# Weight operands of the up projection's first two output tiles formed during the input projection and kept in memory; the sample's residual loaded behind a group of shares

## The chip, the cores and the metric

The kernel runs on one core of a Trainium2 chip. Its engines work side by side: TensorE (PE, with its weight loads as PEld), VectorE (DVE), ScalarE (ACT), GpSimd (POOL) and SyncE (SP, which mostly issues transfers). Each has a queue of its own that it works through in order. The metric is the device time of one launch in microseconds.

## The reference

One layer of a decoder trunk, for a prompt of 1024 tokens and a sample group of 8 sequences with 8 tokens each, 1088 columns in all, in float32. The model width is 1024.

```python
h = rms_norm(x, norm1) * (1 + scale1) + shift1
z = h @ w_in              # q, kc, vc, ks, vs, kw, vw, gates, conv inputs, pooling input
...                       # compressed, selected and window attention; short convolution; pooling
x = x + gate1 * (concat([o_attn, y_conv, y_pool]) @ w_out)
h = rms_norm(x, norm2) * (1 + scale2) + shift2
a, b = split(h @ w_up, 2)                    # w_up: 1024 x 5632
x = x + gate2 * ((silu(a) * b) @ w_down)     # w_down: 2816 x 1024
```

The compressed attention needs the past keys and values, read from a paged cache: blocks of 32 positions go through `silu(flat @ w1) @ w2`.

## The kernel before

Channels lie on the partitions, columns on the free axis. A float32 product is made as three TensorE products of rounded parts: each operand is split into `hi` (a ScalarE copy, line 165) and `lo = operand - hi` (a VectorE subtraction, line 161), and hi x hi, lo x hi and hi x lo are summed in one bank (line 136).

The two big stages of the feed-forward part and the output projection use a scheme with seven products for eight blocks (`PRODUCTS`, `DOWN_PRODUCTS`). For the up projection one output tile j has a weight block of two 512 KB halves `w_raw` (from `in_wup`). From its four quarters seven weight operands are made: two are quarters as they stand, five are sums or differences of two (`w_s`, on GpSimd or VectorE), and each of the seven is split into `w_hi` and `w_lo` (`unit_weights`, seven pieces of 128x512, nine buffers). The columns go in two halves p0 and p1, each with its own operands `b_hi` and `b_lo`, again partly from sums `b_t` (on GpSimd): 7 operands for each of 4 channel groups, 28 per half. A pass (j, p) is 7 products x 4 channel groups x 3 = 84 matmuls of 128x272.

`ffn` makes the passes in the order (0,p0), (1,p0), (2,p0), (2,p1), (1,p1), (0,p1), then (3,p0), (3,p1), (4,p0) and so on. Passes in a row with the same j form a run and share weights, so the first runs are: run 0 = j 0 at p0, run 1 = j 1 at p0, run 2 = j 2 at p0 and p1, run 3 = j 1 at p1, run 4 = j 0 at p1. Tiles 0 and 1 are thus loaded and formed twice. The pieces of run n + 1 are formed during run n. p0's columns are ready first; p1's norm (`n_ss` on line 161, `n_rs` on 1472, `x1b` on 1478 to 1485) and operands come while p0's passes run. The combination of the products is `f_m`, `f_v`, `f_g` (lines 1557 to 1587).

The input projection goes tile by tile, in the order kc, vc, cg0, ch0, bg0, cg1, ch1, bg1, p0, ks, kw, p1, q0 to q3 (here p0 and p1 are two tiles of pooling input, not the halves of the columns). A tile is 24 matmuls for each of three column ranges. Between them a planner written in the kernel weaves in other work: `compress_more` (the compression: SP and GpSimd gather cache pages into `stream`, sixteen `stream` matmuls per step, then `vt`, a silu on ScalarE, and `vt,c_w`) and `late_ada` (`wada` loads and matmuls). The planner keeps an estimated time per engine and emits the step that it thinks ready first; `hold` lets a tile loop wait in the planner while other steps are emitted, and `spawn` starts such a step with a lead. The emitted order is the order of each engine's queue. Behind a pooling tile come running sums on VectorE (`pe_s`, `pe_x`, lines 837 to 857), the product `pe_x,pw` on TensorE, and `py` on ScalarE (line 866), stored to `mix_d`.

In the down projection each product ends in a share: ScalarE writes `d_m` (`down_share`, line 1768) and GpSimd adds it to `x`, or VectorE adds it directly (`down_gate`, line 1758). `down_run` loads the residual of the prompt in four pieces `x2[c]` on SP (line 1821) and that of the sample, `x2s`, on ScalarE's queue:

```python
if e == 1 and h == p == 0:
    nc.scalar.dma_start(xs, self.x1_d[:, :, SEQ:])     # line 1843
```

`issue_after` binds an instruction to stand behind another one in the emitted order.

## Time and profile before

| | before |
|---|---|
| median of 3 runs | 1695.42 us (1692.73 to 1697.64) |
| profiled execution | 1697.3 us |
| its span in the trace | 1695.7 us |
| granted TensorE clock, mean | 0.982 of full speed |
| busy: TensorE / VectorE / ScalarE / GpSimd | 1605.4 / 1122.6 / 819.0 / 680.1 us |

The span runs from the first to the last recorded instruction; 1.6 us of the execution's time lie outside it. The stages stand at these places of the span: input projection about 83 to 366 us, attention to 822, output projection to about 945, up projection to 1446, down projection to the end. The granted clock is the part of full speed that TensorE was given; its two levels are 1.2 and 2.4 GHz, and a stretch at 0.77 is a mix of them.

### The profile page before, as it was taken

What the parts mean: (1) busy time and instruction counts of PE and PEld (TensorE: products, weight loads), DVE (VectorE), ACT (ScalarE), POOL (GpSimd) and SP (SyncE); (2) the same over time, 40 slices, a digit from 0 to 9 for tenths busy, and PEclk for the clock granted to TensorE, in tenths of its full rate; (3) what the DMA queues carried; (4) which work ended last, traced back from release to release, by engine and by line L of the source; (5) the groups of instructions that cost most, each with busy time, mean ns of one, the idle gap of its engine ahead of it and who ended that gap; (6) DMA issues with size and microseconds to landing.
All of it is one profiled execution on the core that took longest, in us unless ns stands there. A gap on an engine that the chain in (4) does not pass through costs nothing.

```text
span 1695.7 us, 34350 instructions
## 1 busy us (share of the span) xinstructions
PE 1605.4 (95%) x11961; PEld 1409.9 (83%) x11961; DVE 1122.6 (66%) x2852; ACT 819.0 (48%) x1884; POOL 680.1 (40%) x797
## 2 busy tenths in 40 slices
PE   6999999998998999999899879999999999899988
PEld 2999997887766566666599769999999999899988
DVE  4603326685664866767689987776777776477695
ACT  3512225245766767666675644433333333344462
POOL 3101110022332322232216486544555554688695
PEclk9999999998999999999999989999999999999999
DMA  9555565216654644432673224436444445967553
GB/s 339 175 190 178 154 207 156 70 63 196 191 168 135 199 130 143 140 111 84 205 247 113 70 70 142 162 132 218 144 142 144 144 144 198 357 256 260 191 170 120
DMA packets 177327, 282.11 MB, mean 166 GB/s; under 512 B 25297, under 2 KB 113938, under 8 KB 176834
## 3 DMA queue, kind: packets, MB, share of 16 engines
q1 hardware_dynamic: 157282, 252.28, 45.5%
q0 software_dynamic: 5856, 16.24, 3.0%
q10 hardware_dynamic: 14016, 11.41, 2.2%
q8 instruction: 95, 1.56, 0.4%
q14 instruction: 78, 0.64, 0.1%
HBM read 220.85 MB, written 63.19 MB: 168 GB/s over the span
## 4 chain that ended last, share of the span: by engine, by line
PE 70%; DVE 12%; DMA 6%; ACT 4%; issue 3%; POOL 2%; SPq 1%; ACTq 0%; POOLq 0%; DVEq 0%
PE bank L136 65%; PE bank L140 5%; DVE w_lo L161 3%; DVE b_lo L161 1%; DMA wada<-in_wada 1%; DMA stream<-in_cacheA 1%; SPq L518 1%; DVE x L1758 1%; DMA w_raw<-in_wup 1%; POOL w_s L161 1%; DVE n_ss L161 1%; ACT w_hi L165 1%; DMA stream<-in_wtok 1%; DMA w_raw<-in_wout 1%; ACT stream L151 1%
## 5 line engine op out<-in xcount | busy, mean ns | idle before, releaser
L136 PE MATMUL bank<-b_hi,w_hi 128*128 128x272 f32 x1232 | 354.5, 293 | 12.9 <-DVE f_v L1557 4.6
L136 PE MATMUL bank<-b_lo,w_hi 128*128 128x272 f32 x1232 | 355.7, 290 | 3.2 <-DVE b_lo L161 3.2
L136 PE MATMUL bank<-b_hi,w_lo 128*128 128x272 f32 x1232 | 351.0, 290 | 1.3 <-DVE w_lo L161 1.3
L136 PEld LDWEIGHTS bank<-b_hi,w_hi 128*128 128x128 f32 x1232 | 232.5, 190 | 18.7 <-ACT b_hi L165 5.1
L136 PEld LDWEIGHTS bank<-b_lo,w_hi 128*128 128x128 f32 x1232 | 234.3, 190 | 4.8 <-DVE b_lo L161 4.6
L136 PEld LDWEIGHTS bank<-b_hi,w_lo 128*128 128x128 f32 x1232 | 232.3, 190 | 2.5 <-DVE w_lo L161 2.3
L1051 POOL TENSOR_SCALAR P<-P,st 128x128 f32<-128x128 f32 (+12 forms) x192 | 112.1, 593 | 262.3 <-DVE st L1049 87.3
L161 DVE TENSOR_TENSOR w_lo<-w_raw,w_hi 128x512 fp32r<-128x512 f32 (+2 forms) x129 | 125.2, 978 | 94.7 <-ACT w_hi L165 94.1
L161 POOL TENSOR_TENSOR w_s<-w_raw 128x512 f32<-128x512 f32 (+1 forms) x106 | 149.6, 1412 | 71.2 <-DVE w_lo L161 53.5
L165 ACT ACTIVATE w_hi<-w_raw 128x512 fp32r<-128x512 f32 (+2 forms) x130 | 86.4, 674 | 138.3 <-PE bank L136 88.5
L161 DVE TENSOR_TENSOR w_lo<-w_s,w_hi 128x512 fp32r<-128x512 f32 (+1 forms) x144 | 134.7, 940 | 19.5 <-ACT w_hi L165 15.1
L136 PE MATMUL bank<-stream 128*128 128x128 f32 x1056 | 133.5, 284 | 7.0 <-DMA stream<-in_cacheA 6.7
L136 PEld LDWEIGHTS bank<-stream 128*128 128x128 f32 x1056 | 128.1, 198 | 14.2 <-issue 9.7
L161 POOL TENSOR_TENSOR x<-x,d_m 128x272 f32<-128x272 f32 x144 | 125.6, 894 | 35.7 <-DVE x L1758 22.9
L136 PE MATMUL bank<-h_hi,w_hi 128*128 128x384 f32 (+1 forms) x384 | 130.8, 341 | 2.4 <-ACT py L866 2.3
L136 PE MATMUL bank<-g,w_hi 128*128 128x272 f32 x616 | 122.3, 294 | 8.4 <-ACT d_m L1768 6.7
L1043 ACT ACTIVATE P<-P,st 128x128 f32<-128x128 f32 (+12 forms) x192 | 113.2, 591 | 30.3 <-DVE st L1034 15.6
L136 PE MATMUL bank<-h_hi,w_lo 128*128 128x384 f32 (+1 forms) x384 | 127.2, 331 | 0.0
L136 PE MATMUL bank<-h_lo,w_hi 128*128 128x384 f32 (+1 forms) x384 | 126.7, 330 | 0.0
L136 PE MATMUL bank<-g,d_hi 128*128 128x272 f32 x616 | 118.7, 290 | 3.7 <-DVE x L1758 3.1
L165 ACT ACTIVATE w_hi<-w_s 128x512 fp32r<-128x512 f32 (+1 forms) x144 | 88.5, 620 | 66.6 <-PE bank L136 36.0
L1758 DVE SCALAR_TENSOR_TENSOR x<-bank,mod,x 128x272 f32<-128x272 f32 (+1 forms) x192 | 87.2, 476 | 42.2 <-PE bank L136 34.5
(369 smaller groups left out, 3855.0 us busy)
## 6 DMA issues: line engine op xcount, KB each, us to landing
g_d<-f_s SPq DMA_DIRECT2D x57, 544.0 KB, 3.4
g<-g_d SPq DMA_DIRECT2D x56, 544.0 KB, 7.9
wada<-in_wada SPq DMA_DIRECT2D x96, 256.0 KB, 5.5
stream<-in_cacheA SPq DMA_DIRECT2D x192, 128.0 KB, 3.4
w_raw<-in_wup SPq DMA_DIRECT2D x48, 512.0 KB, 4.3
unit<-in_cacheB SPq DMA_DIRECT2D x152, 128.0 KB, 2.4
stream<-in_cacheB SPq DMA_DIRECT2D x104, 128.0 KB, 2.3
w_raw<-in_wout SPq DMA_DIRECT2D x24, 512.0 KB, 4.9
```

The source lines that it names most:

```text
L136: return self.nc.tensor.matmul(out, lhsT, rhs, start=start, stop=stop, skip_group_check=chain)
L140: self.nc.tensor.transpose(out, in_, self.ident)
L151: self.nc.scalar.activation(out, in_, AF.Copy)
L161: (self.nc.vector if eng == "dve" else self.nc.gpsimd).tensor_tensor(out, a, b, op=op)
L165: self.nc.scalar.activation(hi, src, AF.Copy)
L518: eng.dma_start(dst[:, a + j, :], self.i[name][bass.ds(regs[j], 1)].rearrange("n p f -> (n p) f"))
L1043: nc.scalar.activation(Ps, Ps, AF.Exp, scale=-1.0, bias=sy[:, 0:1], accum_out=sy[:, 1:2])
L1051: nc.gpsimd.tensor_scalar(Ps, Ps, sy[:, 3:4], 0.0, op0=OP.mult, op1=OP.add)
L1758: nc.vector.scalar_tensor_tensor(out[:, :n], acc[:, :n], self.mod[:, 5, m, 0:1], out[:, :n], op0=OP.mult, op1=OP.add)
```

## The change

- `up_weights_ahead` loads the weight block of tile j, forms its seven pieces and stores them to a tile `w_d` in device memory: seven stores of 512 KB. Tile 0 is formed beside kc and vc, tile 1 beside q0 to q3. A hold behind each (`formed`) keeps the next tiles back until its steps have been emitted.
- `unit_weights` loads `w_hi` and `w_lo` of tiles 0 and 1 from `w_d`, 256 KB each, in place of loading and forming them: runs 0, 1, 3 and 4, 56 loads.
- kw comes behind p1, and the pooling of p1 has to be done before q0.
- The load of `x2s` is bound behind the last share that was emitted before it. On ScalarE it then stands behind the 24 shares of the first group of the down projection, where it stood behind two.

```diff
+AHEAD_W = 2
...
-        order = ["kc", "vc", "cg0", "ch0", "bg0", "cg1", "ch1", "bg1", "p0", "ks", "kw", "p1", "q0", "q1", "q2", "q3"]
+        order = ["kc", "vc", "cg0", "ch0", "bg0", "cg1", "ch1", "bg1", "p0", "ks", "p1", "kw", "q0", "q1", "q2", "q3"]
...
-            yield from tiles(["kc", "vc"], kcv)
+            with self.pool("pre") as pp:
+                self.spawn(0.6, self.up_weights_ahead(pp, 0))
+                yield from tiles(["kc", "vc"], kcv)
+                yield from self.hold(lambda: self.formed == 1)
             nc.gpsimd.dma_start(self.o["kcvcT"], self.kcv)
...
             with self.pool("pooling") as pl:
                 self.pooled = 0
-                for j, names in ((0, ["ks", "kw"]), (1, ["q0", "q1", "q2", "q3"])):
+                for j, names in ((0, ["ks"]), (1, ["kw"])):
                     step = self.pooling_steps(pl, j)
                     yield from tiles(["p" + str(j)], lambda nm, ch, acc, c0, n: step(ch, acc))
                     yield from tiles(names, qk)
                     yield from self.hold(lambda: self.pooled > j)
-                yield from self.hold(lambda: self.prompt_at and self.pooled == 2 and self.heads == 18 and 5 in self.ada_at)
+            with self.pool("pre") as pp:
+                self.spawn(0.6, self.up_weights_ahead(pp, 1))
+                yield from tiles(["q0", "q1", "q2", "q3"], qk)
+                yield from self.hold(lambda: self.formed == 2)
+            yield from self.hold(lambda: self.prompt_at and self.heads == 18 and 5 in self.ada_at)
...
+    def up_weights_ahead(self, pool, j):
+
+        nc = self.nc
+        raw = pool.tile([P, 2, D], F32, name="p_raw")
+        for x in range(2):
+            nc.sync.dma_start(raw[:, x], self.i["wup"][j, x])
+        at = self.use("dma", 2.9, self.t["pe"]) + 2.0
+        src = self.up_operands(raw[:, 0], raw[:, 1])
+        last = None
+        for y, x in enumerate(PRODUCTS):
+            yield at
+            t = pool.tile([P, 2, 512], F32R, name="p_hl", bufs=2)
+            v = src[x][0]
+            if len(src[x]) == 3:
+                v = t[:, 1].bitcast(F32)
+                at = self.combine(v, *src[x], 512, at, "pool")
+            at = self.split(t[:, 0], t[:, 1], v, 512, at)
+            if last:
+                nc.sync.dma_start(*last)
+            last = (self.w_d[j, :, y], t.bitcast(F32))
+        yield at
+        nc.sync.dma_start(*last)
+        self.formed += 1
...
-    def unit_weights(self, wp, j, raw, out):
+    def up_operands(self, ra, rb):
...
+    def unit_weights(self, wp, n, raw, out):
...
+        if isinstance(raw[n], int):
+            for y in range(7):
+                parts = [wp.tile([P, 512], F32R, name=nm, bufs=9) for nm in ("w_hi", "w_lo")]
+                for x in range(2):
+                    nc.sync.dma_start(parts[x].bitcast(F32), self.w_d[raw[n], :, y, x])
+                out.append((*parts, self.use("dma", 1.45, self.t["pe"]) + 2.0))
+                yield
+            return
...
-                raw[n] = tuple(self.weight_load(wp, self.i["wup"][runs[n][0], x]) for x in range(2))
+                j = runs[n][0]
+                raw[n] = j if j < AHEAD_W else tuple(self.weight_load(wp, self.i["wup"][j, x]) for x in range(2))
...
                     if e == 1 and h == p == 0:
-                        nc.scalar.dma_start(xs, self.x1_d[:, :, SEQ:])
+                        with self.tc.issue_after(self.last_share.ins):
+                            nc.scalar.dma_start(xs, self.x1_d[:, :, SEQ:])
...
+        self.w_d = self.dram.tile([AHEAD_W, P, 7, 2, 512], F32, name="w_d")
+        self.formed = 0
```

`up_operands` holds the table of sums and differences that `unit_weights` had.

How the change moves instructions is shown at three places, before and after. The names in brackets are the engines and transfer queues that an instruction waits for. The first place is TensorE behind the tile vc. Before: a step of the compression, `wada`, then the tile cg0 (`h_hi`, `h_lo`).

```order
L136 MATMUL bank<-stream 128x128 [waits DMAHW1_49,DMAHW2_49,DMAHW0_49,DMAHW7_49,DMASW7_49,DMASW0_49]
L136 MATMUL bank<-stream 128x128 x15
L136 MATMUL bank<-wada,sc 32x256 [waits DMAHW6_49]
L136 MATMUL bank<-wada,sc 32x256 [waits DMAHW7_49]
L136 MATMUL bank<-wada,sc 32x256 [waits DMAHW0_49]
L136 MATMUL bank<-wada,sc 32x256 [waits DMAHW1_49]
L136 MATMUL bank<-wada,sc 32x256 x4
L136 MATMUL bank<-h_hi_98,w_hi 128x384 [waits Activation_49]
L136 MATMUL bank<-h_lo_99,w_hi 128x384
L136 MATMUL bank<-h_hi_98,w_lo 128x384 [waits DVE_49]
L136 MATMUL bank<-h_hi_98,w_hi 128x384
L136 MATMUL bank<-h_lo_99,w_hi 128x384
```

After: two more tiles of `stream` with their transfers, `vt,c_w` with a wait for ScalarE, and the next `wada` stand ahead of cg0. The rows follow on the same first `stream` and `wada`.

```order
L137 MATMUL bank<-wada,sc 32x256 x4
L137 MATMUL bank<-stream 128x128 [waits DMAHW3_49,DMAHW2_49,DMAHW4_49,DMASW2_49,DMASW1_49]
L137 MATMUL bank<-stream 128x128 x15
L137 MATMUL bank<-stream 128x128 [waits DMAHW1_49,DMAHW0_49,DMAHW4_49,DMASW5_49,DMAHW5_49,DMASW4_49,DMAHW6_49,DVE_49,DMAHW7_49,PE_49,Activation_49]
L137 MATMUL bank<-stream 128x128 x14
L137 MATMUL bank<-vt,c_w_82 64x256 [waits Activation_49]
L137 MATMUL bank<-vt,c_w_82 64x256 x3
L137 MATMUL bank<-stream 128x128
L137 MATMUL bank<-wada,sc 32x256 [waits DMAHW2_49]
L137 MATMUL bank<-wada,sc 32x256 [waits DMAHW3_49]
L137 MATMUL bank<-wada,sc 32x256 [waits DMAHW4_49]
L137 MATMUL bank<-wada,sc 32x256 [waits DMAHW5_49]
```

What moved: 31 `stream` matmuls and `vt,c_w` from behind cg0 to a place ahead of it. The second place is TensorE around p1's pooling product `pe_x,pw`. Before it stands inside the q tiles.

```order
L136 MATMUL bank<-h_lo_101,w_hi 128x384
L136 MATMUL bank<-h_hi_100,w_lo 128x384
L136 MATMUL bank<-pe_x,pw 128x384 [waits DVE_49,Activation_49]
L136 MATMUL bank<-pe_x,pw 128x384 [waits DVE_49]
L136 MATMUL bank<-pe_x,pw 128x256 [waits DVE_49,PE_49]
L136 MATMUL bank<-pe_x,pw 128x64
L136 MATMUL bank<-h_sq,mean_h 128x384 [waits DVE_49,Activation_49]
```

After, it stands behind kw's last rows and ahead of q0's first.

```order
L141 MATMUL bank<-ident,ada_s 128x128 [waits PE_49,Activation_49]
L141 MATMUL bank<-ident,ada_s 128x128
L137 MATMUL bank<-ksq,mean_h 128x64 [waits Activation_49]
L141 MATMUL bank<-ident,vcT 64x128 [waits DVE_49]
L137 MATMUL bank<-pe_x,pw 128x384 [waits DMAHW4_49,DVE_49,Activation_49]
L137 MATMUL bank<-pe_x,pw 128x384 [waits PE_49]
L137 MATMUL bank<-pe_x,pw 128x256 [waits Activation_49]
L137 MATMUL bank<-pe_x,pw 128x64
L137 MATMUL bank<-h_hi_98,w_hi 128x384 [waits DVE_49,PE_49]
L137 MATMUL bank<-h_lo_99,w_hi 128x384
```

What moved: the product has kw in place of q0 and most of q1 between the pooling tile and itself. The third place is SP at the end of the output projection. Before: loads of `in_wup` between stores of the new residual (`x_d<-x1b`), which wait for VectorE.

```order
L1450 DMA x_d<-x1b 128x272 [waits DMAHW1_49,DVE_49]
L1450 DMA x_d<-x1b 128x272 [waits DMAHW2_49,DVE_49]
L1450 DMA x_d<-x1b 128x272 [waits DMAHW3_49,DVE_49]
L1380 DMA w_raw<-in_wup 128x1024 [waits DMAHW5_49,DMAHW4_49,Pool_49]
L1450 DMA x_d<-x1b 128x272 [waits DVE_49]
L1380 DMA w_raw<-in_wup 128x1024 [waits DMAHW6_49,Activation_49]
L1450 DMA x_d<-x1b 128x272 [waits DMAHW7_49,DVE_49]
L1450 DMA x_d<-x1b 128x272 [waits DMAHW0_49,DVE_49]
```

After: pairs of loads from `w_d`, which wait for TensorE to be done with a buffer, between the same stores.

```order
L1482 DMA x_d<-x1b 128x272 [waits DMAHW4_49,DVE_49]
L1482 DMA x_d<-x1b 128x272 [waits DMAHW5_49,DVE_49]
L1568 DMA w_hi<-w_d 128x512 [waits DMAHW6_49,PE_49]
L1568 DMA w_lo<-w_d 128x512 [waits DMAHW7_49,PE_49]
L1568 DMA w_hi<-w_d 128x512 [waits DMAHW0_49,PE_49]
L1568 DMA w_lo<-w_d 128x512 [waits DMAHW1_49,PE_49]
L1482 DMA x_d<-x1b 128x272 [waits DMAHW2_49,DVE_49]
L1482 DMA x_d<-x1b 128x272 [waits DMAHW3_49,DVE_49]
L1568 DMA w_hi<-w_d 128x512 [waits DMAHW4_49,PE_49]
L1568 DMA w_lo<-w_d 128x512 [waits DMAHW5_49,PE_49]
```

What moved: in place of one load of 512 KB for a half block come two of 256 KB for each product.

## Rows read from the trace of the kernel before

**Rows 1.** Part 1 of the page of the profile: busy time of each engine, its share of the span, and its instructions.

```profile
PE 1605.4 (95%) x11961; PEld 1409.9 (83%) x11961; DVE 1122.6 (66%) x2852; ACT 819.0 (48%) x1884; POOL 680.1 (40%) x797
```

**Rows 2.** Six stretches (in us from the span's start) from the end of the output projection through the up projection: length; busy time and instructions of PE, PEld, DVE, ACT and POOL; PE's granted clock; the busy share of the DMA engines; GB/s.

```profile
925.00:945.00 20.00, 14.33 (x112) 14.02 (x110) 17.96 (x32) 7.74 (x18) 11.07 (x10) 0.95 0.29 94
945.00:985.00 40.00, 33.52 (x217) 30.70 (x216) 40.00 (x76) 25.08 (x53) 23.39 (x18) 0.88 0.18 60
985.00:1005.00 20.00, 16.49 (x97) 15.18 (x97) 16.81 (x26) 8.95 (x22) 18.89 (x20) 0.77 0.12 43
1005.00:1060.00 55.00, 50.98 (x390) 49.00 (x388) 44.73 (x69) 23.50 (x47) 33.36 (x28) 1.00 0.39 130
1060.00:1190.00 130.00, 127.36 (x1004) 125.98 (x1004) 93.99 (x148) 50.60 (x102) 64.19 (x57) 1.00 0.50 174
1190.00:1446.00 256.00, 255.24 (x2031) 254.28 (x2031) 182.98 (x289) 99.60 (x201) 130.04 (x118) 1.00 0.44 155
```

**Rows 3.** One line of the waits from 985 to 1005 us: who waited, on which line, for what; us in total, times, the longest in us.

```profile
ACT b_hi L165 <- POOL b_t L161: 5.2, 7, 1.6
```

**Rows 4.** The chain that ended last, from 940 to 1062 us: start in us, length in us, what.

```profile
983.36 8.60 PE bank L136 x51
...
1003.83 1.51 DVE b_lo L161
```

**Rows 5.** VectorE's instructions grouped by shape, from 925 to 985 us and (the last two lines) from 985 to 1060 us: line, operation, output and inputs, count; busy us and mean ns; idle time before them.

```profile
L161 DVE TENSOR_TENSOR w_lo<-w_s,w_hi 128x512 fp32r<-128x512 f32 x15 | 12.4, 828 | 0.1
L161 DVE TENSOR_TENSOR b_lo<-b_t,b_hi 128x272 fp32r<-128x272 f32 x11 | 9.7, 878 | 0.0
...
L161 DVE TENSOR_TENSOR w_lo<-w_raw,w_hi 128x512 fp32r<-128x512 f32 x6 | 5.7, 948 | 0.1
...
L161 DVE TENSOR_TENSOR w_lo<-w_s,w_hi 128x512 fp32r<-128x512 f32 x20 | 21.6, 1093 | 0.0
...
L161 DVE TENSOR_TENSOR w_lo<-w_raw,w_hi 128x512 fp32r<-128x512 f32 x8 | 8.5, 1059 | 3.1 <-ACT w_hi L165 3.1
```

**Rows 6.** GpSimd's instructions grouped by shape, from 925 to 1060 us, and single instructions of VectorE in order of time (start in us, length in us): operand splits `b_lo` and a weight split `w_lo`.

```profile
L161 POOL TENSOR_TENSOR w_s<-w_raw 128x512 f32<-128x512 f32 x29 | 41.7, 1441 | 27.9 <-DVE w_lo L161 22.2 <-DMA w_raw<-in_wup 5.6
L161 POOL TENSOR_TENSOR b_t<-x1b 128x272 f32<-128x272 f32 x20 | 20.9, 1064 | 8.5 <-ACT x1b L1485 4.3 <-DVE x1b L1483 2.7 <-DVE b_lo L161 1.5
...
960.74 0.43 DVE L161 TENSOR_TENSOR b_lo<-x1b,b_hi 128x272 fp32r<-128x272 f32 x1
...
968.59 0.68 DVE L161 TENSOR_TENSOR w_lo<-w_s,w_hi 128x512 fp32r<-128x512 f32 x1
...
1007.66 0.43 DVE L161 TENSOR_TENSOR b_lo<-b_t,b_hi 128x272 fp32r<-128x272 f32 x1
```

**Rows 7.** TensorE in order of time, at the end of the output projection (start, length; in brackets the idle time before it and what ended it).

```profile
944.26 1.25 PE L136 MATMUL bank<-n_ss,mean_d 128*128 128x272 f32 x2 [5.67 <-DVE n_ss L161]
```

**Rows 8.** One stretch at the change from up to down projection; columns as in rows 2.

```profile
1446.00:1453.00 7.00, 1.27 (x8) 1.05 (x7) 1.21 (x3) 0.86 (x2) 6.52 (x9) 0.90 1.07 394
```

**Rows 9.** Two stretches of the input projection; columns as in rows 2.

```profile
83.00:113.00 30.00, 30.00 (x212) 28.33 (x211) 2.38 (x5) 4.43 (x10) 2.16 (x4) 1.00 0.55 176
...
306.00:366.00 60.00, 60.00 (x350) 54.91 (x347) 45.26 (x45) 16.31 (x33) 3.43 (x8) 1.00 0.18 46
```

**Rows 10.** The compression in the input projection: TensorE's `stream` and `wada` matmuls in order of time, SP's issue of a tile's six gathers, transfers from 70 to 130 us (count, KB each, median us from issue to landing), and ScalarE's share of the silu ahead of `vt,c_w`.

```profile
113.33 3.73 PE L136 MATMUL bank<-stream 128*128 128x128 f32 x32
117.00 1.07 PE L136 MATMUL bank<-wada,sc 128*32 128x256 f32 x16
...
100.48 2.94 SPq L518 DMA_DIRECT2D stream<-in_cacheA  x6
...
wada<-in_wada SPq DMA_DIRECT2D x16, 256.0 KB, 3.9
stream<-in_cacheA SPq DMA_DIRECT2D x18, 128.0 KB, 4.9
w_raw<-in_win SPq DMA_DIRECT2D x4, 512.0 KB, 4.9
...
130.20 0.27 ACT L571 ACTIVATE vt<-bank 64x128 f32<-64x128 f32 x1 [3.08 <-PE bank L136]
...
134.69 0.72 ACT L610 ACTIVATE vt<-pre,pec 128x512 f32<-128x512 f32 x1
```

**Rows 11.** The pooling: the first and the last VectorE instruction of p1's chain, and TensorE's wait behind p0's.

```profile
306.89 1.42 DVE L837 TENSOR_TENSOR pe_s<-pe_x 128x1222 f32<-128x1222 f32 x1
...
322.08 0.17 DVE L857 COPY pe_x<-pe_f 64x16 f32<-64x16 f32 x1
...
266.77 0.44 PE L136 MATMUL bank<-h_hi,w_hi 128*128 128x384 f32 x1 [2.31 <-ACT py L866]
```

**Rows 12.** The change from up to down projection in order of time: TensorE, then ScalarE with its queue (ACTq), then VectorE.

```profile
1452.24 0.82 PE L136 MATMUL bank<-g,w_hi 128*128 128x272 f32 x2 [5.73 <-ACT d_m L1768]
...
1451.10 0.55 ACTq L1843 DMA_DIRECT2D x2s<-x_d  x1
1451.70 0.86 ACT L1768 ACTIVATE d_m<-bank,mod 128x272 f32<-128x272 f32 x2 [9.19 <-POOL f_T L161]
...
1451.31 0.48 DVE L1876 MEMSET x<- 128x512 f32 x1 [8.47 <-DMA x<-x_d]
...
1453.90 0.91 DVE L1758 SCALAR_TENSOR_TENSOR x<-bank,mod,x 128x272 f32<-128x272 f32 x2 [1.38 <-DMA x<-x_d]
```

More of the change, by code (lines that the diff above doesn't have):

```diff
@@ L1519, in operands @@
         yield 0.0
-    def unit_weights(self, wp, j, raw, out):
-        nc = self.nc
-        while j not in raw:
-            yield 0.0
-        (ra, ta), (rb, tb) = raw[j]
+    def up_operands(self, ra, rb):
         A11, A12 = ra[:, 0:512], ra[:, 512:1024]
         A21, A22 = rb[:, 0:512], rb[:, 512:1024]
-        src = {4: (A22,), 5: (A11, A12, OP.add), 2: (A21, A22, OP.add), 1: (A11, A22, OP.add), 3: (A11,),
-               7: (A12, A22, OP.subtract), 6: (A21, A11, OP.subtract)}
+        return {4: (A22,), 5: (A11, A12, OP.add), 2: (A21, A22, OP.add), 1: (A11, A22, OP.add), 3: (A11,),
+                7: (A12, A22, OP.subtract), 6: (A21, A11, OP.subtract)}
+    def unit_weights(self, wp, n, raw, out):
+        nc = self.nc
+        while n not in raw:
+            yield 0.0
+        if isinstance(raw[n], int):
[6 more added lines that the diff above has]
+            return
+        (ra, ta), (rb, tb) = raw[n]
+        src = self.up_operands(ra, rb)
         for x in PRODUCTS:
```

## The prediction

> **What bounds the kernel now.** The page comes first. TensorE is busy for 95% of the span [rows 1], so a change can only win where TensorE waits, or lose by making it wait somewhere new. The second view cuts the end of the span into stretches. From 1190 to 1446 us the up projection does 2031 matmuls in 256.00 us, 0.126 us each, and this is the pace that TensorE can keep. At that pace the other stretches [rows 2] lose: 925 to 945 us 20 - 112 x 0.126 = 5.9 us; 945 to 985 us 12.7; 985 to 1005 us 7.8; 1005 to 1060 us 5.9; 1060 to 1190 us 3.5. So 32.3 us are lost from 925 to 1060 us, where the first runs of the up projection stand, and almost nothing behind it. The granted clock there falls to 0.88 and 0.77, and is 1.00 from 1005 us on; that lies inside the loss.
>
> What TensorE waits for is in the waits, the chain and the rows of single instructions. VectorE is busy for all 40.00 us from 945 to 985 us [rows 2]. In 985 to 1005 us ScalarE's `b_hi` waits 5.2 us for GpSimd's `b_t` [rows 3]; the chain goes over TensorE alone for 8.60 us and then comes back to a `b_lo` [rows 4]. So the prompt's second half p1 is late: its last `b_lo` ends at 1008.1 us [rows 6], and before it the p0 passes of three runs are all that TensorE has. VectorE's time there is split between these operands and weights: 15 + 6 `w_lo` (18.1 us) against 11 `b_lo` of sums (9.7 us) from 925 to 985 us, and 20 + 8 `w_lo` (30.1 us) from 985 to 1060 us [rows 5]. 49 pieces are seven runs of 7.
>
> **The change, part by part.** *Weights taken out of the up projection.* Runs 0, 1, 3 and 4 lose 28 `w_lo`, 28 `w_hi` and 20 combines. Runs 0 and 1 stand ahead of the last `b_lo`: 14 `w_lo` at (12.4 + 5.7)/21 = 0.86 us are 12.1 us of VectorE. Their 10 combines leave GpSimd, 10 x 1.441 = 14.4 us [rows 6], and VectorE is slower beside GpSimd: `b_lo` takes 0.88 us in the mean against 0.43 us in a row that runs alone, `w_lo` 0.83 to 1.09 against 0.68 [rows 5, 6]. How much of these 14.4 us VectorE gets back no row shows; between 0 and all of it I take a third, 5, because VectorE is busy with other things for much of a combine. The last `b_lo` then ends 17 us sooner, at 991 us.
>
> The Trainium skill ("SBUF — State Buffer", section "SBUF: two separate sides") says that GpSimd and a VectorE operation with two SBUF inputs take their shared port pair as an exclusive lock and that the loser waits for the whole instruction. That speaks for giving back nearly all of the 14.4 us; by it the last `b_lo` would stand near 984 us.
>
> TensorE starts the up projection at about 945 us, after 5.67 us of waiting for VectorE's `n_ss` [rows 7]. Three p0 passes of 84 matmuls take 31.8 us, so p1 is wanted from 976 us on, and the seventh product, six times 1.5 us later, at 985 us. Against 991 us a wait of 6 us stays; I add 3 for the start at a lower clock. Of the 20.5 us lost from 945 to 1005 us, 11.5 are won. From 1005 to 1060 us runs 3 and 4 form nothing any more: 4.5 of 5.9. From 925 to 945 us `n_ss` stands behind fewer pieces: 4 of 5.9. Sum: **20 us won**. The upper bound is the whole loss, 32. The lower one is 8.5, if only the last two come: GpSimd's 20 `b_t` of 1.064 us [rows 6] and p1's own norm are not touched.
>
> *The loads that take their place.* A product needs 512 KB in 84 x 0.126/7 = 1.5 us, 347 GB/s; 394 GB/s were moved in 1446 to 1453 us [rows 8]. The nine buffers run up to 13.5 us ahead, and runs 0 and 1 pass in 21 us what two runs need. The pairs stand on SP behind stores of p1's `x1b`, which wait for VectorE; those end early enough for product after product, so I put it at nothing. If the cover goes, p0's passes stretch towards p1's operands, which are late anyway: at most 6 us.
>
> *Forming in the input projection, first time.* 1 MB comes in and 3.67 MB go out during kc and vc. VectorE is busy for 2.38 us of 30, ScalarE 4.43, GpSimd 2.16 [rows 9]: seven `w_lo` of 0.95 us, seven splits and five combines of 1.44 us fit [rows 5, 6]. The transfers make 176 GB/s at a share of 0.55 into 176/0.55 = 320 where the share is full, so the 4.7 MB take 15 of these 30 us: close to full. TensorE does not read any of it. But the hold ahead of cg0 lets the compression go first. Where cg0 stood behind sixteen `stream` matmuls, 31 more of them, `vt` and eight `wada` stand now, and cg0 behind. The second sixteen are there by then. The next need the tile that the first sixteen free at 117.1 us: gathers of 2.94 us, landing 4.9 us after the last one at most, so until 124.9, while TensorE has work (1.07 us of `wada` and 3.73 of `stream`) until 121.8: 3.1 us of waiting [rows 10]. Then `vt`: from the last `stream` matmul at 130.2 us to the end of silu at 135.4 us ScalarE and VectorE take 5.2 us [rows 10], now with nothing of TensorE's beside it. Together **8 us**; between 4, if the tile is there and half of the silu hidden, and 17, if the `wada` behind it (3.9 us to land) and cg0's weights (4.9) come one after the other.
>
> *Second time, with q0 to q3, and p1 ahead of kw.* Forming itself is hidden: VectorE is busy for 45 of 60 us there, and 7 `w_lo` fit. What is late next is p1's pooling, whose `pw` product now stands between kw and q0. On VectorE that chain lasts from 306.9 to 322.3 us, 15.4 us, and for cover TensorE has kw, 72 matmuls at 60.00/350 = 0.171 us, 12.3 us [rows 9, 11]: 3 us of waiting. Behind it ScalarE's `py`, which wait for one another's stores, stand ahead of the next `w_hi`; the trace has 2.31 us for such a wait [rows 11], of which I take 1, since q0 covers most. **4 us**; bounds 0 and 10, with three such waits in full. Nothing comes back: TensorE is busy all through 83 to 113 us and 306 to 366 us [rows 9].
>
> *The residual's load.* It holds ScalarE until 1451.10 us, and `d_m` behind it starts at 1451.70. TensorE stands from 1446.5 to 1452.24 us for that `d_m` [rows 12]. Two products, 12 matmuls, stand there (2.7 us at half clock, to 1454.9); behind them TensorE needs VectorE's `x`, whose loads land at 1451.3 and 1453.9 us [rows 12] in both kernels, so 1453.90 + 0.5 = 1454.4 us at best. Without the wait the two products are done before that: **0.6 us** won, between 0 and the whole wait of 5.7.
>
> **Sum.** 1697.3 - 20 + 8 + 4 - 0.6 = 1688.7 us by the profiled run, which stands 1.9 us above the median of 1695.4. Against the median that is 1686.8, so 1687 us. The attention is planned anew around the moved work; no row prices that, and it goes into the range.
>
> **The rivals.** *Forecast* (chance 0.48), 1680 to 1693 us. *p1's operands are no earlier* (0.20): GpSimd's `b_t` and p1's norm set the time, as ScalarE's 5.2 us of waiting for `b_t` [rows 3] suggests; against it stands VectorE, without an idle us from 945 to 985 [rows 2]. The up projection wins 8.5 us, and the kernel takes 1687 + 11.5 = 1698.5. *The hold empties TensorE's queue* (0.15), the one on the other side: tile refill, silu, `wada` and cg0's weights stand one behind the other, 17 us, and `pw` and the first q tiles 10 us, together 27 instead of 12: 1702 us. It decides from 26 us on, 5 more than the up projection and the residual give. For it speaks the DMA share near full with the stores; against it, that ScalarE and VectorE are idle there. *The combines hold VectorE* (0.17): with all 14.4 us back the last `b_lo` ends at 1008.1 - 14 x 0.68 - 14.4 = 984 us and p1's 6 us go: 1681 us, and down to 1671 where the other 6 us of the loss and the tile refill go too. The port rule of the Trainium skill ("SBUF — State Buffer") gives this one. That `w_lo` stretches to 1.09 us and not by a whole combine is what the trace has against it.
>
> That the change doesn't take the forming away can't be: four runs have loads in place of splits.
>
> **Range and chances.** 1671 to 1703 us holds all but the outer part of the last two cases. A measurement of this kernel tells a difference from none at about 0.3%, 5 us: faster is below 1690.3, slower above 1700.5. Faster: 0.40 of the forecast's 0.48 and 0.17, 0.57. Slower: 0.15 and 0.05 of the second case, 0.20. Within: 0.23.
>
> **What would show it.** In the profile after: in the first 60 us of the up projection fewer than 25 `w_lo` on VectorE, the last `b_lo` some 17 us sooner after the first up matmul, and the loss from there to 1060 us down from 26 to about 10. TensorE idle before `stream` and `vt,c_w` behind vc (8 us) and before `pe_x,pw` (3 us). The residual's load off ScalarE's wait at 1451 us, and TensorE's stop there only a little shorter. The prediction is wrong if the waits behind vc are over 15 us, if loads of `w_hi` and `w_lo` end TensorE's waits, or if `b_lo` is as late as before.

## The result, and the profile after

| | before | after |
|---|---|---|
| median | 1696.47 us (1692.73 to 1697.64, 4 runs) | 1684.85 us (1682.07 to 1686.67, 4 runs) |
| span of the profiled execution | 1695.7 us | 1685.1 us |
| ratio, with its 95% interval | | 0.9934 [0.9912, 0.9955] |

By the medians the change makes the kernel 11.6 us faster; by the ratio it is 0.66%. Forecast were 1687 us and a ratio of 0.995. From the first matmul of one stage to that of the next the traces give:

| us | before | after |
|---|---|---|
| input projection, from kc's first matmul to q3's last | 280.7 | 288.4 |
| attention | 472.5 | 473.2 |
| output projection | 100.4 | 100.8 |
| up projection, to the first matmul of the down projection | 500.4 | 478.8 |
| down projection | 253.6 | 253.1 |

The up projection wins 21.6 us, and what lies ahead of the attention takes 10.1 us back: 7.7 us in the input projection, and 2.4 because kc itself starts later, at 85.7 us. That start isn't shown to be the change's: with the input projection of the kernel before, kc starts at 83.0 us in one of the traces below and at 86.8 in another.

The windows that answer to [rows 2], 12 us later, since the up projection starts 11 us later. Columns as there.

```profile
937.00:957.00 20.00, 20.00 (x159) 19.84 (x158) 16.01 (x38) 9.03 (x22) 3.48 (x5) 1.00 0.82 279
957.00:997.00 40.00, 33.32 (x240) 31.83 (x238) 37.04 (x71) 21.55 (x51) 27.14 (x28) 0.95 0.32 114
997.00:1017.00 20.00, 19.88 (x137) 19.43 (x137) 8.93 (x20) 5.74 (x14) 3.85 (x5) 0.85 0.90 315
1017.00:1072.00 55.00, 54.85 (x439) 54.63 (x438) 46.12 (x68) 24.33 (x49) 35.01 (x31) 1.00 0.48 170
```

At 0.126 us a matmul they lose 0.0, 9.8, 2.7 and -0.3 us: 12.2, where before lost 32.3. The seven `w_lo` that VectorE still makes there, the `b_lo`, and GpSimd's sums, from 936 to 1001 us:

```profile
L162 DVE TENSOR_TENSOR b_lo<-b_t,b_hi 128x272 fp32r<-128x272 f32 x26 | 17.3, 688 | 1.2 <-ACT b_hi L166 1.2
L162 DVE TENSOR_TENSOR b_lo<-x1b,b_hi 128x272 fp32r<-128x272 f32 x8 | 6.5, 845 | 0.0
L162 DVE TENSOR_TENSOR w_lo<-w_s,w_hi 128x512 fp32r<-128x512 f32 x5 | 4.0, 793 | 0.0
L162 DVE TENSOR_TENSOR w_lo<-w_raw,w_hi 128x512 fp32r<-128x512 f32 x2 | 1.4, 687 | 0.2 <-ACT w_hi L166 0.2
...
L162 POOL TENSOR_TENSOR b_t<-x1b 128x272 f32<-128x272 f32 x20 | 18.9, 964 | 17.6 <-ACT x1b L1517 14.0 <-DVE b_lo L162 1.9 <-DVE x1b L1515 1.7
L162 POOL TENSOR_TENSOR w_s<-w_raw 128x512 f32<-128x512 f32 x4 | 5.5, 1367 | 10.5 <-DVE w_lo L162 10.5
```

The last `b_lo` ends at 1001.0 us, 53.0 us behind the up projection's first matmul at 948.0; before it was 1008.1 - 936.9 = 71.2. That is 18.2 us sooner (17 were forecast). The prediction put the up projection's start at 945 us; the trace has it at 936.9, with twelve matmuls ahead of the wait for `n_ss`. The first up matmul before, and the first up matmul and the last `b_lo` after:

```profile
936.92 0.29 PE L136 MATMUL bank<-b_hi,w_hi 128*128 128x272 f32 x1
...
948.05 0.29 PE L137 MATMUL bank<-b_hi,w_hi 128*128 128x272 f32 x1
...
999.87 1.14 DVE L162 TENSOR_TENSOR b_lo<-b_t,b_hi 128x272 fp32r<-128x272 f32 x3
```

Most of what the input projection pays stands behind vc: TensorE, then VectorE and ScalarE, then SP's issue, in order of time; the windows that answer to [rows 9]; and last the window from 113 to 139 us before.

```profile
120.28 3.84 PE L137 MATMUL bank<-stream 128*128 128x128 f32 x32
129.49 5.05 PE L137 MATMUL bank<-stream 128*128 128x128 f32 x30 [5.37 <-DVE pre L540]
134.47 0.66 PE L137 MATMUL bank<-vt,c_w 64*64 64x256 f32 x8
...
129.43 0.06 DVE L540 MEMSET pre<- 128x2 f32 x1 [2.16 <-ACT vt L611]
...
124.15 0.27 ACT L572 ACTIVATE vt<-bank 64x128 f32<-64x128 f32 x1 [7.11 <-PE bank L137]
...
128.64 0.72 ACT L611 ACTIVATE vt<-pre,pec 128x512 f32<-128x512 f32 x1
...
121.27 3.30 SPq L519 DMA_DIRECT2D stream<-in_cacheA  x6
...
83.00:113.00 30.00, 30.00 (x210) 28.33 (x210) 6.30 (x12) 7.37 (x15) 7.32 (x8) 0.97 0.89 304
113.00:139.00 26.00, 20.63 (x170) 18.47 (x170) 3.72 (x9) 5.51 (x11) 3.79 (x7) 0.93 0.70 219
...
113.00:139.00 26.00, 26.00 (x199) 24.27 (x198) 4.36 (x8) 7.00 (x13) 2.71 (x5) 1.00 0.68 222
```

The third tile of `stream` waits in one piece, 5.37 us, and it ends with the silu of the step before it (ScalarE to 129.36, then VectorE's fill of the next `pre`). Behind it `vt,c_w` doesn't wait. The granted clock is 0.93 there; before, the whole stretch was busy at 1.00. The forming itself lies beside kc and vc, with the transfers at 0.89 in place of 0.55.

The change from up to down projection, as in [rows 12]: TensorE, ScalarE, VectorE.

```profile
1442.73 0.82 PE L137 MATMUL bank<-g,w_hi 128*128 128x272 f32 x2 [5.09 <-DVE x L1802]
...
1437.69 0.49 ACT L1812 ACTIVATE d_m<-bank,mod 128x272 f32<-128x272 f32 x1 [0.27 <-PE bank L137]
...
1441.09 0.48 DVE L1921 MEMSET x<- 128x512 f32 x1 [8.72 <-POOL f_T L162]
```

ScalarE isn't held any more, and TensorE now waits for VectorE's `x`: 5.09 us in place of 5.73.

### The profile page after: what moved, and what is told of

Read it like the earlier page. It is cut to its first block, busy times and chain, and to the rows that moved or that the text cites. A ratio compares the mean times of both kernels' runs of the same rounds, so it can differ in the third digit from the quotient of the medians.

```text
span 1685.1 us, 34456 instructions
## 1 busy us (share of the span) xinstructions
PE 1605.7 (95%) x11961; PEld 1414.9 (84%) x11961; DVE 1121.4 (67%) x2854; ACT 806.1 (48%) x1852; POOL 665.6 (39%) x789
## 4 chain that ended last, share of the span: by engine, by line
PE 78%; DVE 9%; DMA 4%; ACT 3%; issue 2%; POOL 2%; SPq 1%; ACTq 0%; DVEq 0%; POOLq 0%
PE bank L137 72%; PE bank L141 6%; DVE w_lo L162 1%; DMA w_raw<-in_wup 1%; SPq L519 1%; DVE x L1802 1%; DMA mixc<-mix_d 1%; DVE h_sq L754 1%; DVE b_lo L162 1%; ACT stream L152 1%; DVE x L454 1%; POOL w_s L162 1%; DVE h_lo L463 0%; ACT w_hi L166 0%; DVE d_lo L162 0%
## 5 line engine op out<-in xcount | busy, mean ns | idle before, releaser
L1083 POOL TENSOR_SCALAR P<-P,st 128x128 f32<-128x128 f32 (+11 forms) x192 | 112.7, 596 | 258.2 <-DVE st L1081 99.1
L162 DVE TENSOR_TENSOR w_lo<-w_raw,w_hi 128x512 fp32r<-128x512 f32 (+2 forms) x121 | 117.5, 981 | 53.5 <-ACT w_hi L166 53.0
L162 POOL TENSOR_TENSOR w_s<-w_raw 128x512 f32<-128x512 f32 (+1 forms) x88 | 125.5, 1426 | 64.8 <-DVE w_lo L162 52.7
L166 ACT ACTIVATE w_hi<-w_raw 128x512 fp32r<-128x512 f32 (+2 forms) x122 | 81.4, 678 | 131.8 <-PE bank L137 85.1
L1075 ACT ACTIVATE P<-P,st 128x128 f32<-128x128 f32 (+11 forms) x192 | 113.1, 590 | 29.2 <-DVE st L1066 17.7
L162 DVE TENSOR_TENSOR w_lo<-w_s,w_hi 128x512 fp32r<-128x512 f32 (+1 forms) x124 | 116.0, 938 | 15.3 <-ACT w_hi L166 13.0
L137 PEld LDWEIGHTS bank<-g,w_hi 128*128 128x128 f32 x616 | 98.1, 191 | 9.5 <-DVE x L1802 7.0
```

The lines of the kernel that those rows point to most:

```text
L137: return self.nc.tensor.matmul(out, lhsT, rhs, start=start, stop=stop, skip_group_check=chain)
L162: (self.nc.vector if eng == "dve" else self.nc.gpsimd).tensor_tensor(out, a, b, op=op)
L166: self.nc.scalar.activation(hi, src, AF.Copy)
L1075: nc.scalar.activation(Ps, Ps, AF.Exp, scale=-1.0, bias=sy[:, 0:1], accum_out=sy[:, 1:2])
L1083: nc.gpsimd.tensor_scalar(Ps, Ps, sy[:, 3:4], 0.0, op0=OP.mult, op1=OP.add)
```

## The experiments

The runs are from three chips, with 4 to 12 executions each. Every ratio is to the kernel before on the same chip, whose median was 1698.4 to 1699.8 us; a difference in us is worked out from the ratio, and where two runs are from different chips they are compared by their ratios.

**The three parts of the change, one by one.** Form only:

```diff
-                raw[n] = j if j < AHEAD_W else tuple(self.weight_load(wp, self.i["wup"][j, x]) for x in range(2))
+                raw[n] = tuple(self.weight_load(wp, self.i["wup"][j, x]) for x in range(2))
```

> All of the changed kernel stays except that the up projection loads and forms the weights of tiles 0 and 1 itself, as before; the stored pieces are not read. So it pays for the input projection and wins nothing in the up projection. By the prediction's terms: +8 behind vc, +4 around the pooling product, -0.6 for the residual, so 1696.5 + 11.4 = 1708 us. By the profile after, which shows 10.1 us more up to the last q matmul: 1706. If the profile of the changed kernel shows a wait that the up projection's missing work has caused in part (the rival that the input projection costs nothing by itself): within 3 us of before. If the attention gives back some of it: about 1701.

Measured 1.0084 [1.0068, 1.0100], +14.3 us. The up projection takes 500.6 us in its trace, as before. So the work ahead is paid without the up projection's part in it, and 3 us more than by the terms of the sum. In its trace the input projection takes 290.5 us, 9.8 more than before, and the attention 476.2, 3.7 more.

Load only (on the kernel before, with `unit_weights` of the changed one):

```diff
+        self.w_d = self.dram.tile([P, 2, 512], F32, name="w_d")
...
+                    nc.sync.dma_start(parts[x].bitcast(F32), self.w_d[:, x])
```

> The kernel before, with its input projection, but runs 0, 1, 3 and 4 of the up projection load their operands (always the same 512 KB piece, stored once from another tile) and form nothing. Its values in the feed-forward part are therefore not the model's. By the prediction's terms: -20 us, 1676. By the profile after (up projection 21.6 us shorter from its first matmul to the down projection's first): 1675. Rival, p1's operands are no earlier without the work ahead: -8.5, 1688. Together with the run that forms only, the two should add up to the changed kernel to within 2 us if the parts don't touch each other.

Measured 0.9894 [0.9879, 0.9910]. The four times lay between 1671.9 and 1683.0 us, so it was run again:

> The run that loads only, once more beside the others, as its four times lay 11 us apart and its sum with the run that forms only missed the changed kernel by 8 us. If the parts add up: form only +14.3, changed kernel -11 to -13, so -25 to -27 us against before, ratio 0.985. If they don't: 0.9894 again.

Measured 0.9882 [0.9865, 0.9899], -20.1 us: the forecast's 20. In both traces the up projection takes 477 us, as in the changed kernel, and the last `b_lo` ends 52.6 and 52.8 us behind its first matmul.

The residual alone, on the kernel before:

```diff
-                        nc.scalar.dma_start(xs, self.x1_d[:, :, SEQ:])
+                        with self.tc.issue_after(self.last_share.ins):
+                            nc.scalar.dma_start(xs, self.x1_d[:, :, SEQ:])
```

> The kernel before with the sample's residual bound behind the shares, and nothing else. Prediction: -0.6 us, so no difference that a measurement tells (ratio 0.9996). Rival, the load held ScalarE's shares and with them TensorE: -5.7 us, ratio 0.9966.

Measured 1.0002 [0.9990, 1.0013]: no difference. TensorE's wait there is 5.47 us and ends with VectorE's `x`, as in the changed kernel.

The changed kernel once more, beside other runs:

> The changed kernel itself, beside the others of this call, so that they can be compared with it on one chip. From the first comparison: ratio 0.9934. If the two parts just add up (form only 1.0084, load only 0.9894): 0.998.

Measured 0.9932 [0.9913, 0.9951], the first result again. By their ratios the parts add to 14.3 - 20.1 = -5.8 us, where the whole gives -11.5; each of the three has an interval of about 3 us to either side. In the traces most of the gap lies in the attention: it takes 476 us in the run that forms only and in the second that loads only, and 472.5 to 473.2 in the kernel before and twice in the changed one. The order of TensorE's instructions there differs between the kernel before and the changed one, but the run that forms only has the changed kernel's order, and both that load only have the order of before; yet the first of these two takes 471.0 us and the second 475.9. So the difference comes without any change of order, and why the attention takes the one time or the other is **open**.

**What takes VectorE's time in the up projection.** Before, with the ten combines of runs 0 and 1 left out:

```diff
-            if len(src[x]) == 3:
+            if len(src[x]) == 3 and j > 1:
                 t = wp.tile([P, 512], F32, name="w_s", bufs=2)
```

> The kernel before, but the ten sums and differences of the weights of runs 0 and 1 are left out: each of those pieces is split from one quarter, so ScalarE's and VectorE's splits stay and only the combines go; the feed-forward values are not the model's. It measures how much of VectorE's time the combines on GpSimd take. Prediction's term (a third of 14.4 us comes back): last b_lo about 5 us sooner after the up projection's first matmul, kernel about 4 us faster, 1692.5. Rival, a combine holds VectorE for its whole length: 14 us sooner, kernel 9 to 12 us faster, 1686. Rival, nothing comes back: 1696.

Measured 0.9963 [0.9951, 0.9976], -6.3 us. The last `b_lo` ends 67.8 us behind the first up matmul, 3.4 sooner than before. So the combines give back a fourth of their 14.4 us at that place, and the rival in which they hold VectorE for their whole length has fallen. The order has moved with it: all seven pieces of run 3 stand ahead of that `b_lo`, where five did before, and the two take 2.3 us, so the combines alone are worth some 5.7 us there (an estimate). The two splits and the last `b_lo`:

```profile
1005.69 0.68 DVE L161 TENSOR_TENSOR w_lo<-w_s,w_hi 128x512 fp32r<-128x512 f32 x1
...
1006.64 1.65 DVE L161 TENSOR_TENSOR w_lo<-w_s,w_hi 128x512 fp32r<-128x512 f32 x1
...
1008.56 1.47 DVE L161 TENSOR_TENSOR b_lo<-b_t,b_hi 128x272 fp32r<-128x272 f32 x1
```

The rest of the gain lies where the forecast hadn't put it; the window around the up projection's start (942.2 us here) is that of 925 to 945 us before:

```profile
930.00:950.00 20.00, 19.97 (x156) 19.62 (x155) 17.00 (x35) 10.72 (x23) 5.13 (x5) 1.00 0.32 102
```

It loses 0.3 us in place of 5.9: TensorE's wait for `n_ss` is gone without any split being gone. GpSimd's work there is 5.13 us against 11.07. Run 0's seven splits begin from 20 to 2 us ahead of the first up matmul, where they began from 18 us ahead of it to 3 us behind it. Whether `n_ss` came sooner because VectorE was stretched less or because of this other order isn't shown.

Only runs 0 and 1 load, runs 3 and 4 form:

```diff
-                raw[n] = j if j < AHEAD_W else tuple(
+                raw[n] = j if j < AHEAD_W and n < 2 else tuple(
```

> The changed kernel, but only runs 0 and 1 of the up projection load their operands; runs 3 and 4 form them again. It splits the 20 us. Prediction's terms: 4.5 us of the gain belong to runs 3 and 4, so 4 to 5 us slower than the changed kernel, ratio to before 0.996. By the windows after (1005 to 1060 us lost 5.9 before and nothing after): 6. Rival, the gain is in the first two runs alone: no slower than the changed kernel, 0.993.

Measured 0.9989 [0.9974, 1.0004]: 9.7 us slower than the changed kernel. Its up projection takes 488.4 us. Its windows that answer to those from 957 to 1072 us after the change, and VectorE's `w_lo` from 939 to 1010 us:

```profile
959.00:999.00 40.00, 34.42 (x244) 32.83 (x242) 37.42 (x73) 22.09 (x50) 25.73 (x25) 0.91 0.27 95
999.00:1019.00 20.00, 16.02 (x86) 15.29 (x86) 17.48 (x25) 10.07 (x22) 13.97 (x13) 0.66 0.16 53
1019.00:1074.00 55.00, 52.55 (x414) 51.70 (x412) 43.61 (x69) 23.99 (x48) 33.39 (x30) 1.00 0.47 167
...
L162 DVE TENSOR_TENSOR w_lo<-w_s,w_hi 128x512 fp32r<-128x512 f32 x8 | 8.2, 1028 | 0.0
L162 DVE TENSOR_TENSOR w_lo<-w_raw,w_hi 128x512 fp32r<-128x512 f32 x4 | 4.4, 1096 | 0.2 <-ACT w_hi L166 0.2
```

They lose 9.3, 9.2 and 2.8 us. Of the twelve `w_lo`, seven are run 2's and five run 3's. They stand ahead of the last `b_lo`, which ends 59.1 us behind the first up matmul: 12.1 us sooner than before, and 6.1 later than with all four runs loaded. The five pieces of run 3 stood there in the kernel before too, ahead of its last `b_lo` (1007.66 us in [rows 6]):

```profile
983.14 0.90 DVE L161 TENSOR_TENSOR w_lo<-w_raw,w_hi 128x512 fp32r<-128x512 f32 x1
983.96 1.25 DVE L161 TENSOR_TENSOR w_lo<-w_s,w_hi 128x512 fp32r<-128x512 f32 x1
...
1001.48 2.43 DVE L161 TENSOR_TENSOR w_lo<-w_s,w_hi 128x512 fp32r<-128x512 f32 x2
...
1005.26 1.77 DVE L161 TENSOR_TENSOR w_lo<-w_raw,w_hi 128x512 fp32r<-128x512 f32 x1
```

All three first tiles formed ahead, beside q0 to q3 (both late, as below, with `AHEAD_W = 3`):

> Both tiles formed beside q0 to q3, and tile 2 with them: 21 pieces there, and run 2 of the up projection loads too. Theory A, weights on VectorE still hold p1's operands: 7 w_lo and 4 combines less, last b_lo 6 us sooner, 5 of the 12 us that the up projection still loses are won; the third tile's forming takes 21 x 3.3 = 70 us against 54 us of q tiles, so 5 to 15 us are lost there: 0 to 10 us slower than with two tiles late. Theory B, p1's own norm and sums on ScalarE and GpSimd set the time now (GpSimd idles 14.0 us for x1b there): last b_lo no sooner, nothing won, and the loss behind q3 stays.

Measured 0.9954 [0.9938, 0.9970], by the ratios 11.6 us slower than with two tiles late (below), a little outside the forecast's 0 to 10. The last `b_lo` ends 44.1 us behind the first up matmul, 9 sooner than after the change, and the up projection takes 467.6 us, 10 to 11 less:

```profile
970.00:1010.00 40.00, 39.02 (x302) 37.91 (x302) 34.49 (x75) 21.38 (x52) 24.20 (x26) 1.00 0.73 248
```

302 matmuls in 40 us lose 1.9. So the weights (splits on VectorE with their combines on GpSimd) were still what held p1, and not its own norm (theory A). The price is behind q3, where forming outlasts the q tiles and the gathers behind the hold come late; TensorE's waits from 366 to 400 us:

```profile
PE bank L137 <- DMA stream<-in_cacheA: 12.7, 1, 12.7
PE bank L137 <- DVE sel L319: 3.1, 1, 3.1
```

From q3's last matmul to the output projection it takes 493.2 us, 20 more.

**What the input projection pays for.** Both tiles formed beside q0 to q3, no hold behind vc:

```diff
-            with self.pool("pre") as pp:
-                self.spawn(0.6, self.up_weights_ahead(pp, 0))
-                yield from tiles(["kc", "vc"], kcv)
-                yield from self.hold(lambda: self.formed == 1)
+            yield from tiles(["kc", "vc"], kcv)
...
-                self.spawn(0.6, self.up_weights_ahead(pp, 1))
+                self.spawn(0.6, self.up_weights_both(pp))
```

`up_weights_both` forms tile 0 and then tile 1.

> The changed kernel with both tiles formed beside q0 to q3, so that no hold stands behind vc and cg0 keeps its place. Theory (the hold behind vc costs 7 to 8 us of waiting, 5.37 of them one wait): 8 us less there; the second forming takes twice as long and 14 pieces at 3 to 4 us (two store buffers) run past the 54 us of q0 to q3, so up to 5 come back: 3 to 8 us less than the changed kernel. Rival, the cost is the transfers and the lower granted clock and not the order: no gain against the changed kernel.

Measured 0.9886 [0.9868, 0.9904], 1678.4 us: 7.2 us less than the changed kernel beside it (1685.6). Behind vc TensorE is busy all through again, at full clock:

```profile
113.00:139.00 26.00, 26.00 (x200) 24.52 (x199) 3.26 (x8) 6.56 (x12) 2.71 (x5) 1.00 0.59 192
```

The hold behind vc is gone and so is its cost. The transfers moved away with it; that they are not the cost is shown below, in the run with ks as cover. Next, q0 as more cover for p1's pooling:

```diff
-                for j, names in ((0, ["ks"]), (1, ["kw"])):
+                for j, names in ((0, ["ks"]), (1, ["kw", "q0"])):
...
-                yield from tiles(["q0", "q1", "q2", "q3"], qk)
+                yield from tiles(["q1", "q2", "q3"], qk)
```

> The changed kernel with q0 put between kw and the second forming, so that p1's pooling has kw and q0 for cover, 26 us in place of 12.3. Prediction's term for the second place: 4 us less than the changed kernel. By the profile after, where the waits around that product sum to under 2 us: 0 to 2 us less.

Measured 0.9915 [0.9897, 0.9933], 1683.4 us, 2.2 less than the changed kernel: under the forecast's 4, and not clear of its interval.

Two other orders keep a tile behind each hold. The first puts ks and kw beside the first forming, q0 behind p0, q1 behind p1, and leaves q2 and q3 for the second forming:

> The changed kernel with its tiles in another order: kc, vc, ks, kw beside the first forming, then the conv tiles, p0, q0, p1, q1, and q2, q3 beside the second forming. Each hold then has its cover in a tile that TensorE works on. Theory (the holds empty TensorE's queue, 8 us at the first and 1 to 4 us at the second): 9 to 12 us less than the changed kernel. Rival, the cost is the transfers and the clock: within 2 us of it.

Measured 0.9910 [0.9891, 0.9928], 4.1 us less. The 113 to 139 us are full in its trace too, but from 320 to 376 us TensorE waits 4.3 us at once for p1's pooling. The wait:

```profile
342.31 4.09 PE L137 MATMUL bank<-pe_x,pw 128*128 128x384 f32 x8 [4.26 <-DVE pe_x L858]
```

Part of what the one end gains is lost at the other. This run therefore doesn't speak for its rival, by which transfers and clock are the cost behind vc; it leaves that rival undecided.

The second has ks beside the first forming, kw behind p0, q0 behind p1, and three tiles for the second forming (the moved start of the compression, which now comes ahead of ks, is left out here):

```diff
+        order = ["kc", "vc", "ks", "cg0", "ch0", "bg0", "cg1", "ch1", "bg1", "p0", "kw", "p1", "q0", "q1", "q2", "q3"]
...
+                yield from tiles(["kc", "vc"], kcv)
...
+                yield from tiles(["ks"], qk)
+                yield from self.hold(lambda: self.formed == 1)
...
+                for j, names in ((0, ["kw"]), (1, ["q0"])):
...
+                yield from tiles(["q1", "q2", "q3"], qk)
```

> The changed kernel with another order of tiles, so that every hold has a tile as cover: ks beside the first forming, kw behind p0, q0 behind p1, q1 to q3 beside the second forming. Theory (TensorE's waits come from the holds): the 7 us behind vc go, as in the run with both tiles formed late, and the 2 us that q0 as cover for p1's pooling gave; 9 us less than the changed kernel, ratio to before about 0.988. Rival, 2 MB stay in the same stretch as kc and vc and the transfers and the clock take some of it: 4 us less, as in the run with ks and kw there, ratio 0.991.

Measured 0.9876 [0.9860, 0.9892], 1678.2 us: 21 us faster than before and 9.5 faster than the changed kernel, where the theory had 9. Its input projection takes 280.0 us in the trace (280.7 before). The first forming stays beside kc and vc, and TensorE pays nothing for it that the trace shows:

```profile
83.00:113.00 30.00, 30.00 (x212) 28.33 (x211) 6.21 (x11) 7.38 (x15) 7.31 (x8) 1.00 0.87 296
113.00:139.00 26.00, 26.00 (x199) 24.06 (x198) 11.03 (x14) 8.90 (x15) 3.80 (x7) 1.00 0.68 212
```

The transfers are as dense as after the change (0.87 against 0.89), the clock is 1.00, and TensorE doesn't wait; so neither the transfers nor a clock that they lower is the cost behind vc. This version beats both kernels; so does the one with both tiles late, by nearly as much.

## Why the prediction was right, point by point

- **p1's operands late because of weights on VectorE: right.** The last `b_lo` comes 18.2 us sooner. The rival in which p1's own norm and GpSimd's `b_t` set the time (8.5 us) fell with that, and again with three tiles ahead, where the last `b_lo` came 9 us sooner still.
- **The working behind the 17 us: wrong, and the sum right by luck.** It counted the pieces of runs 0 and 1 alone as standing ahead of the last `b_lo`: 12.1 us for 14 splits and 5 for their combines. With these two runs loaded it came 12.1 us sooner, and only with runs 3 and 4 loaded too 18.2. What the step left out is run 3: its pieces are formed during run 2, whose second pass waits for p1, so five of them stood ahead of the last `b_lo` too, for 6.1 us.
- **The split of the 20 us: wrong.** "From 1005 to 1060 us runs 3 and 4 form nothing any more: 4.5 of 5.9." These two runs were worth 9.7 us, for the reason just given. What runs 0 and 1 win alone is 12 us in the trace (500.4 to 488.4), not 15.5. The two errors cancelled.
- **The loss by stretches: its sum was right, its parts were not.** The terms leave 1.9, 9 and 1.4 us of loss from 925 to 945, 945 to 1005 and 1005 to 1060 us, 12.3 in all. The windows after have 0.0, 12.5 and -0.3. So the stretch in which p1 is late won 8 us, not 11.5, and the two beside it won the rest.
- **925 to 945 us: "4 of 5.9", and all of it came.** The reason given was fewer pieces ahead of `n_ss` on VectorE. The runs show that leaving out the combines alone was enough; how it acts isn't shown.
- **The third of 14.4 us for combines: about right where the combines alone go** (3.4 measured, some 5.7 by the estimate above, against 5), but not seen beside the splits, where runs 0 and 1 gave the 12.1 us of their splits and no more. The page of the Trainium skill that was weighed ("SBUF — State Buffer", section "SBUF: two separate sides") has the loser wait for the whole instruction. Single rows fit that: the split below ends 0.54 us behind the combine's end at 940.52, and the same split takes 0.68 us elsewhere. What doesn't come out is the working from it that gave back nearly all of the 14.4 us; this split paid for what was left of the combine when it started, and not for the whole of it.

```profile
939.26 1.26 POOL L161 TENSOR_TENSOR w_s<-w_raw 128x512 f32<-128x512 f32 x1 [4.00 <-DMA w_raw<-in_wup]
...
939.51 1.55 DVE L161 TENSOR_TENSOR w_lo<-w_s,w_hi 128x512 fp32r<-128x512 f32 x1
```

- **Behind vc, 8 us: the size was right (7.2 by taking the hold away), the working not.** "3.1 us of waiting" for the tile and then 5.2 for the silu were added. The trace shows one wait of 5.37 us, which by the profile the silu's chain ends. The gathers were issued to 124.6 us; 4.9 us to land [rows 10] would put them near 129.5 too (an estimate), so the two run side by side and don't add. The rest of the 7.2 is not waiting at that place; what goes with it in the traces is the clock, 0.93 there and 0.87 in the second trace of the changed kernel: the 30 `stream` matmuls behind the wait take 5.05 us, the 32 ahead of it 3.84.
- **Around p1's pooling, 4 us: too high, or unresolved;** q0 as cover won 2.2 us, with an interval that includes nothing. `pe_x,pw` waits for nothing that the profile shows, and 1.09 us of waiting stand just ahead of it. Together with the place behind vc 12 us were forecast; the input projection takes 7.7 us more in the trace after, and 8.0 to 9.8 in three other runs with the changed kernel's input projection.
- **The loads in place of forming at nothing: right.** In the changed kernel's first 20 us of the up projection they fill 0.82 of the transfers' time, and TensorE is busy for 20.00 us.
- **The residual, 0.6 us: right.** The releaser changes from `d_m` to `x`, and the wait shrinks by 0.64 us (by 0.26 in the run with the residual alone); no measurement here tells it from nothing.
- **Nothing else moved beyond what executions differ by:** attention and output projection differ by 0.7 and 0.4 us in the first two traces, although the planner made a new order around the moved compression. The attention's 471 to 476 us under one order leave room for more.

## What to carry to other kernels

Work that is moved to a stage with idle engines can cost by what its buffers need, and not by its busy time: here a buffer that had to close before the next stage put a hold into the order, and the hold emptied the queue of the engine that was the bound. Put a piece of work of that engine ahead of each such hold, as cover; here one tile was enough, and the same forming then cost nothing that the traces show. And when pieces are taken out ahead of a due point in a queue, count every piece that stands there, also those of a later run: here five of run 3 did.

## What the runs showed that was not expected

- The granted clock of the input projection's first 30 us differs between executions of the same instructions. From 83 to 113 us it was 1.00 in the profile of the kernel before, and 0.94 in that of the kernel with the residual bound, which is the same up to the down projection; TensorE then did 204 matmuls in place of 212.

```profile
83.00:113.00 30.00, 30.00 (x204) 28.34 (x203) 2.51 (x6) 3.94 (x9) 2.15 (x4) 0.94 0.55 182
```

- A wait of TensorE can cost more than its length: in the 26 us that hold the wait of 5.37 us the granted clock was 0.93, and 0.87 in the second trace, and it was 0.66 from 999 to 1019 us in the run with runs 3 and 4 formed, where TensorE was busy for 16.02 of 20 us.
- Ten combines of 1.44 us on GpSimd, which TensorE never reads directly, were worth 6.3 us of the kernel's time, most of it where TensorE waited for `n_ss`.
